# A stick-breaking row's survival product in one scan against a floor tile, and the residual gate's sum moved behind the last such row

## The chip, the cores and the metric

The kernel runs on one core of a Trainium2 chip. The metric is the device time of one execution in microseconds (us): a median of three executions. Engines are named as the profile names them: PE (TensorE, matrix multiplication), DVE (VectorE), ACT (ScalarE), POOL (GpSimd) and SP (SyncE, which here issues DMAs).

## The reference

One layer with two groups of eight heads of 64 columns, over 1024 positions of width 1024. What matters here is the stick-breaking group and the residual's gate:

```python
def _stick_breaking_block(q, k, v, q_pos, k_pos):
    z = einsum('bhqd,bhkd->bhqk', q, k) * scale
    strict = k_pos[None, :] < q_pos[:, None]
    log_beta = log_sigmoid(z)
    log_keep = where(strict, log_sigmoid(-z), 0.0)
    later = cumsum(log_keep, axis=3, reverse=True) - log_keep
    w = where(strict, exp(log_beta + later), 0.0)
    return einsum('bhqk,bhkd->bhqd', w, v)
...
mod = silu(c) @ w_ada + b_ada          # shift, scale, gate: 1024 columns each
u = layer_norm(x) * (1 + scale) + shift
h = u @ w_in                           # q, k, v, g and forget columns of both groups
y = concat([y_fox, y_sb]) @ w_out      # heads' outputs times silu of their g columns
x = layer_norm(2 ** 0.25 * x + gate * y, ln_g, ln_b)
```

The other group, forgetting attention, is an ordinary causal softmax with a bias of cumulated forget gates.

## The kernel before

All matrix products are made of float32 split into a high and a low part (`whi`/`wlo`, `uh`/`ul`, `pt` in two halves), three matmuls for one.

*Start.* The sequence is normalised, and the projection of the first two pairs of heads is made while the modulation is worked out. In this stage, w_gate comes in as eight tiles of 128 x 1024 (`wg`, in the `att` ring of six buffers), and DVE adds them up, each times its element of silu(c), into the tile `gate` (`gate_term`, 16 halves). Two matmuls with a constant 0.5 sum that tile over its partitions, and b_gate is added (`gen_gate`).

*Attention.* Eight pairs of heads follow one another. Pairs 0 to 3 are stick-breaking, pairs 4 to 7 forgetting. A unit is one pair, one head and one block `i` of 128 queries, against (i+1) x 128 keys. For a stick-breaking unit: PE makes the scores S, ACT makes `kp` = sigmoid(-S) and `be` = sigmoid(S), DVE turns `kp` from right to left into the product of all later keeps with two scans, first on the 128 diagonal columns (against `ident`, whose one restarts the product at each row's own position), then on the columns left of them, starting from the first scan's last value. POOL multiplies `be` by the shifted `kp`. Two units later PE transposes the result, ACT and DVE split it (`pt`), and PE multiplies it by v (`pv`). The score tile has one buffer, so the next unit's scores wait for ACT's two sigmoids. For a forgetting unit DVE adds the bias row `fb` and reduces, ACT takes the exponential, DVE inverts the sum and POOL scales the row (`a`).

*Fillers.* Between the units' matmuls PE works through `fillers`, a chain of generators that make the projections of later pairs in small steps (`gen_m`: `m` tiles for q, k or g of a pair, `gen_v`: v of two pairs). `FILL` tells how many steps each pair's units take with them. `beside(main, side)` advances `side` by one step for each step of `main`. `gen_split_out` runs beside pairs 4 to 6: it loads half a block of w_out, multiplies it by `gate` (`raw_o`, L123), splits it (`whi_o` L125, `wlo_o` L126) and stores both parts in DRAM (`wo_dr`), from where `gen_last_g` loads them for the output projection. `SPACE` is the number of steps between two of the 16 halves. All weights pass through two `raw` buffers (`raw_tile`) and a ring of five pairs of `whi`/`wlo` buffers (`RING`).

*Order.* PE's order is that of the code, and SP's is in the start stage; the other queues, and SP later, are ordered by a scheduler. Each engine works through its own queue in order.

Of the kernel before, what the change touches and what calls it, by code (L numbers as in the profile page):

```python
# [13 lines left out]
P = 128  # L14
# [13 lines left out]
def tile_hybrid_layer(  # L28
# [27 lines left out]
    def att_tile(name, dt=F32):  # L56
        return big("att", 6, name, dt)
# [18 lines left out]
    GEARLY = 8  # L76
    NORM_ON = {6: nc.vector, 7: nc.vector}
    FROW = 12
    SPACE = 5
    GATE = 6  # L80
# [23 lines left out]
    gate = cp.tile([P, D], F32, tag="gate", name="gate")  # L104
# [292 lines left out]
    def att_scores(u, following):  # L397
# [28 lines left out]
        else:  # L426
# [6 lines left out]
            rv = kp[:, dg][:, ::-1]  # L433
            nc.vector.tensor_tensor_scan(rv, rv, ident[:, ::-1], initial=0.0, op0=ALU.mult, op1=ALU.max)  # L434
            if i:
                rv = kp[:, :ke - P][:, ::-1]
                nc.vector.tensor_tensor_scan(rv, rv, rv, initial=kp[:, ke - P:ke - P + 1],  # L437
                                             op0=ALU.mult, op1=ALU.min)
# [51 lines left out]
    def chain(gens):  # L490
        for g in gens:
            yield from g
# [179 lines left out]
    wg = {}  # L672

    def load_gate(kt):
        wg[kt] = att_tile(f"wg_{kt}")
        nc.sync.dma_start(wg[kt], w_gate[kt])

    def gate_term(kt, h):
        s = slice(h * 512, h * 512 + 512)
        if kt == 0:  # L680
            nc.vector.tensor_scalar(gate[:, s], wg[kt][:, s], sc[:, 0:1], None, op0=ALU.mult)
        else:
            nc.vector.scalar_tensor_tensor(gate[:, s], wg[kt][:, s], sc[:, kt:kt + 1], gate[:, s],
                                           op0=ALU.mult, op1=ALU.add)

    def gen_gate():
        b = att_tile("bg")
        nc.sync.dma_start(b, b_gate.to_broadcast([P, D]))
        for _ in range(GATE):
            yield  # L690
        for h in range(2):
            s = slice(h * 512, h * 512 + 512)
            gp = t_tile(f"gate_{h}")

            nc.tensor.matmul(gp, half.to_broadcast([P, P]), gate[:, s], start=True, stop=True)
            nc.vector.scalar_tensor_tensor(gate[:, s], b[:, s], 0.5, gp, op0=ALU.mult, op1=ALU.add)
            yield
# [21 lines left out]
    for kb in range(NB):  # L719
        if kb + 2 < NB:  # L720
            rounded = late_round(kb + 2)
        start_steps(range(2), acc1, kb, 512, 1024)
        if kb < 4:
            load_gate(kb)
        if kb < len(evacs):
            n, h = evacs[kb]
            with after(*rounded):
                evac_m(*START[n], 0, acc0[n], (h,))
    acc1 += [pv_tile("st_g0b"), pv_tile("st_q1b"), acc_tile("st_k1b")]
    v0_w.update((n, fetch_w(f"v0_{n}b", w_v[0, n], 512)) for n in (2, 3))  # L730
    for n in range(5):
        if n >= 2:
            for kb in range(NB):
                start_steps((n,), acc1, kb, 512, 1024)
                step = (n - 2) * NB + kb
                if step % 3 == 1 and step // 3 < GEARLY:
                    with after(rounded[1]):
                        gate_term(step // 3, 0)
                        gate_term(step // 3, 1)
                    if step // 3 < 4:  # L740
                        load_gate(step // 3 + 4)
        last_evac = evac_m(*START[n], 1, acc1[n])
# [22 lines left out]
    def gen_split_out():  # L765
        for pr in range(NPAIR):
            for h in range(2):
                s = slice(h * 512, h * 512 + 512)
                hi, lo = fetch_w(f"o{pr}_{h}", w_out[pr * P:(pr + 1) * P, s], 512, gate[:, s])
# [97 lines left out]
    def gen_last_g(p):  # L867
# [14 lines left out]
        beside(chain([gen_v(0, v0_w, range(4, NB)), gen_m(1, 2)]), gen_gate()),  # L882
# [142 lines left out]
```

## Time and profile before

| | |
|---|---|
| executions | 709.02, 707.76, 707.51 us; median 707.76 |
| span of the profiled execution | 705.8 us, clock 0.998 |
| time of the profiled execution itself | not recorded apart from its span; the median lies 1.96 us above it |
| PE / DVE / ACT / POOL busy | 680.8 / 509.6 / 378.8 / 422.4 us |
| first score of attention | 92.6 us |
| first scores of pairs 1, 2, 3, 4 | 148.1, 222.8, 292.1, 361.7 us |
| first scores of pairs 5, 6, 7 | 435.5, 508.1, 571.3 us |

The span runs from the first to the last instruction of one profiled execution. PE is busy for 96% of it, so the interest lies in the few microseconds in which it is not, and in what it waits for then. In the views a group of instructions is named by its line, its engine and operation and the tiles it writes and reads (out<-in), then its count, its busy time, the mean of one in ns, and the engine's idle time just before it with what ended that.

### The profile page before, as it was taken

To read this page: it belongs to the slowest core of one execution; us is meant where nothing else is said; L and a number is where in the kernel's file an instruction comes from. 1 tells how busy PE (TensorE), PEld (TensorE's weight loads), DVE (VectorE), ACT (ScalarE), POOL (GpSimd) and SP (SyncE) were. 2 spreads that over 40 slices of the span, in tenths; PEclk is the share of its full clock that TensorE was granted. 3 is DMA by queue.
4 is the path that set the end of the run, shared out by engine and by line. 5 is a ranking of instruction groups with operands and counts; after the bars stand their busy time and mean duration, and the time that the engine had idled before them with its cause. 6 is when DMAs were issued, how large, how long until landed. Compare 5 with 4: busy or idle time off the path is not lost. (4 is left out here: it accounts for less than half of the span.)

```text
span 705.8 us, 11791 instructions
## 1 busy us (share of the span) xinstructions
PE 680.8 (96%) x4033; PEld 593.0 (84%) x4033; DVE 509.6 (72%) x963; ACT 378.8 (54%) x856; POOL 422.4 (60%) x523
## 2 busy tenths in 40 slices
PE   7999998989999999999999999999999999999995
PEld 4789887878998888889998887889988889888884
DVE  5985689897858697788686685757676767774644
ACT  4667346756658566666665563646564666621000
POOL 4560258665629675857388897868583455665412
PEclk9999999999999999999999999999999999999999
DMA  8953451101101212112034554435241189143301
GB/s 306 415 212 126 132 167 35 28 26 53 53 7 37 70 37 67 43 38 68 9 124 155 176 170 137 134 105 165 92 148 53 56 271 371 48 162 113 121 32 59
DMA packets 44027, 81.59 MB, mean 116 GB/s; under 512 B 5120, under 2 KB 18880, under 8 KB 43072
## 3 DMA queue, kind: packets, MB, share of 16 engines
q1 hardware_dynamic: 42816, 76.65, 32.4%
q10 hardware_dynamic: 1152, 4.19, 2.1%
q8 instruction: 32, 0.52, 0.3%
q14 instruction: 27, 0.22, 0.1%
HBM read 60.34 MB, written 16.29 MB: 109 GB/s over the span
## 5 line engine op out<-in xcount | busy, mean ns | idle before, releaser
L256 PE MATMUL m<-uh,whi 128*128 128x512 f32 x304 | 126.4, 416 | 0.0
L257 PE MATMUL m<-ul,whi 128*128 128x512 f32 x304 | 119.9, 394 | 0.0
L258 PE MATMUL m<-uh,wlo 128*128 128x512 f32 x304 | 119.7, 394 | 0.0
L459 DVE TENSOR_TENSOR pt<-T,pt 128x512 fp32r<-128x512 f32 (+2 forms) x192 | 100.5, 549 | 14.6 <-ACT pt L458 13.3
L439 POOL TENSOR_TENSOR be<-be,kp 128x127 f32<-128x127 f32 (+3 forms) x64 | 79.0, 1235 | 47.0 <-DVE kp L437 44.3
L458 ACT CAST pt<-T 128x512 fp32r<-128x512 f32 (+2 forms) x192 | 85.8, 480 | 18.6 <-PE T L456 14.8
L471 PEld LDWEIGHTS pv<-pt,v 128*128 128x128 f32 x640 | 83.9, 188 | 10.4 <-DVE pt L459 5.2
L471 PE MATMUL pv<-pt,v 128*128 128x256 f32 (+1 forms) x640 | 85.1, 277 | 4.5 <-DVE pt L459 3.6
L437 DVE TENSOR_TENSOR_SCAN kp<-kp 128x128 f32<-128x128 f32 (+6 forms) x56 | 82.6, 1476 | 1.9
L424 POOL TENSOR_SCALAR a<-a,l 128x1024 f32<-128x1024 f32 (+3 forms) x64 | 48.3, 755 | 41.7 <-DVE l L423 28.1
L422 ACT ACTIVATE a<-a,nm 128x1024 f32<-128x1024 f32 (+3 forms) x64 | 49.8, 779 | 40.8 <-DVE nm L417 38.9
L410 PE MATMUL S<-k,q 128*128 128x512 f32 (+5 forms) x192 | 66.8, 349 | 2.3 <-ACT be L430 1.7
L258 PEld LDWEIGHTS m<-uh,wlo 128*128 128x128 f32 x304 | 57.1, 188 | 13.6
L411 PE MATMUL S<-kl,qz 128*128 128x512 f32 (+5 forms) x192 | 65.5, 342 | 0.0
L256 PEld LDWEIGHTS m<-uh,whi 128*128 128x128 f32 x304 | 57.3, 189 | 8.8 <-DVE kl L244 0.4
L257 PEld LDWEIGHTS m<-ul,whi 128*128 128x128 f32 x304 | 57.4, 189 | 8.0
L480 POOL TENSOR_TENSOR ty<-ty,sg 64x256 f32<-64x256 f32 x64 | 48.8, 762 | 19.7 <-DVE ty L479 9.8
L434 DVE TENSOR_TENSOR_SCAN kp<-kp,ident 128x128 f32<-128x128 f32 x64 | 42.0, 656 | 24.4 <-ACT kp L429 21.1
L417 DVE CUSTOM_DVE_ANT_0 a<-S,fb 128x1024 f32<-128x1024 f32 (+3 forms) x64 | 48.2, 754 | 15.7 <-issue 6.5
L429 ACT ACTIVATE kp<-S 128x128 f32<-128x128 f32 (+3 forms) x64 | 41.7, 652 | 32.9 <-PE S L411 31.4
L126 POOL TENSOR_TENSOR wlo<-raw,whi 128x512 fp32r<-128x512 f32 x38 | 56.8, 1496 | 3.4 <-DMA wo_dr<-wlo_o 1.8
L311 PE MATMUL v<-whi_v,uh 128*128 128x256 f32 (+1 forms) x192 | 56.0, 292 | 1.1 <-DVE kl L244 1.1
(280 smaller groups left out, 1633.2 us busy)
## 6 DMA issues: line engine op xcount, KB each, us to landing
raw<-in_w_qkg_dram SPq DMA_DIRECT2D x38, 256.0 KB, 2.7
wss<-in_w_ss_dram SPq DMA_DIRECT2D x7, 1024.0 KB, 8.5
x<-in_x_dram SPq DMA_DIRECT2D x8, 512.0 KB, 7.6
k<-k SPq DMA_DIRECT2D x32, 128.0 KB, 2.2
wg<-in_w_gate_dram SPq DMA_DIRECT2D x8, 512.0 KB, 5.2
raw_o<-in_w_out_dram SPq DMA_DIRECT2D x16, 256.0 KB, 2.6
fb<-f_dr ACTq DMA_DIRECT2D x8, 512.0 KB, 4.2
wo_dr<-whi_o SPq DMA_DIRECT2D x16, 256.0 KB, 2.5
```

Of the source, the lines that this page charges most:

```text
L126: nc.gpsimd.tensor_tensor(lo[:, :n], raw, hi.bitcast(F32)[:, :n], op=ALU.subtract)
L256: nc.tensor.matmul(acc, hi[:, c], u_hi[kt][:, s], start=(kt == 0), stop=False)
L257: nc.tensor.matmul(acc, hi[:, c], u_lo[kt][:, s], start=False, stop=False)
L258: nc.tensor.matmul(acc, lo[:, c], u_hi[kt][:, s], start=False, stop=(kt == NB - 1))
L311: nc.tensor.matmul(acc[:, :n], u_hi[kt][:, ts_], hi[:, s], start=(kt == 0), stop=False)
L410: nc.tensor.matmul(S[:, s, :w], qst[p][h][:, qs], kst[p][h][:, ks], start=True, stop=False)
L411: nc.tensor.matmul(S[:, s, :w], z, klo[p][:, ks], start=False, stop=True)
L437: nc.vector.tensor_tensor_scan(rv, rv, rv, initial=kp[:, ke - P:ke - P + 1], op0=ALU.mult, op1=ALU.min)
L439: nc.gpsimd.tensor_tensor(be[:, :ke - 1], be[:, :ke - 1], kp[:, 1:ke], op=ALU.mult)
L458: nc.scalar.copy(hi[:, :n, qo:qo + P], t3)
L459: nc.vector.tensor_tensor(lo[:, :n, qo:qo + P], t3, hi.bitcast(F32)[:, :n, qo:qo + P], op=ALU.subtract)
L471: nc.tensor.matmul(acc[:, q0:256], vt[p][:, kb, h * P:(h + 1) * P], pt[:, kb % 4, q0:], start=(part == 0 and kb == 0), stop=(part == 1 and ...
```

## The change

The two scans of a stick-breaking row become one over the whole row. Its second operand is a new tile `floor`, 1024 columns wide: zeros, and `ident` in the last 128. The state is multiplied by `kp` and then held at no less than the floor. POOL writes `floor` at the start.

`floor` lies in the buffer of `gate` (both have the tag `gate` in a pool with one buffer). The gate can therefore only be begun when the last stick-breaking scan has read `floor`. The sum moves from the start stage into `gen_gate`, which now runs beside the fillers of pairs 4 and 5: 16 halves of 128 x 512, loaded through the two `raw` buffers, one every `GATE` = 2 steps after `GATE0` = 6 steps, then the two matmuls. `gen_split_out` follows behind it, beside the fillers from pair 6's k on, with `SPACE` 3 instead of 5.

```diff
-    GEARLY = 8
...
-    SPACE = 5
-    GATE = 6
+    SPACE = 3
+    GATE0 = 6
+    GATE = 2
...
-    gate = cp.tile([P, D], F32, tag="gate", name="gate")
+    floor = cp.tile([P, D], F32, tag="gate", name="floor")
+    nc.gpsimd.memset(floor[:, :D - P], 0.0)
+    nc.gpsimd.tensor_copy(floor[:, D - P:], ident)
...
-            rv = kp[:, dg][:, ::-1]
-            nc.vector.tensor_tensor_scan(rv, rv, ident[:, ::-1], initial=0.0, op0=ALU.mult, op1=ALU.max)
-            if i:
-                rv = kp[:, :ke - P][:, ::-1]
-                nc.vector.tensor_tensor_scan(rv, rv, rv, initial=kp[:, ke - P:ke - P + 1],
-                                             op0=ALU.mult, op1=ALU.min)
+            rv = kp[:, :ke][:, ::-1]
+            nc.vector.tensor_tensor_scan(rv, rv, floor[:, D - ke:][:, ::-1], initial=0.0,
+                                         op0=ALU.mult, op1=ALU.max)
...
-    def load_gate(kt):
-        wg[kt] = att_tile(f"wg_{kt}")
-        nc.sync.dma_start(wg[kt], w_gate[kt])
...
     def gen_gate():
-        b = att_tile("bg")
-        nc.sync.dma_start(b, b_gate.to_broadcast([P, D]))
-        for _ in range(GATE):
+        for _ in range(GATE0):
             yield
+        gate = cp.tile([P, D], F32, tag="gate", name="gate")
+        gates.append(gate)
+        for kt in range(NB):
+            for h in range(2):
+                s = slice(h * 512, h * 512 + 512)
+                raw = raw_tile(f"wg_{kt}_{h}")[:, :512]
+                nc.sync.dma_start(raw, w_gate[kt][:, s])
+                if kt == 0:
+                    nc.vector.tensor_scalar(gate[:, s], raw, sc[:, 0:1], None, op0=ALU.mult)
+                else:
+                    nc.vector.scalar_tensor_tensor(gate[:, s], raw, sc[:, kt:kt + 1], gate[:, s],
+                                                   op0=ALU.mult, op1=ALU.add)
+                for _ in range(GATE):
+                    yield
         for h in range(2):
             s = slice(h * 512, h * 512 + 512)
+            b = raw_tile(f"bg_{h}")[:, :512]
+            nc.sync.dma_start(b, b_gate[:, s].to_broadcast([P, 512]))
             gp = t_tile(f"gate_{h}")
             nc.tensor.matmul(gp, half.to_broadcast([P, P]), gate[:, s], start=True, stop=True)
-            nc.vector.scalar_tensor_tensor(gate[:, s], b[:, s], 0.5, gp, op0=ALU.mult, op1=ALU.add)
+            nc.vector.scalar_tensor_tensor(gate[:, s], b, 0.5, gp, op0=ALU.mult, op1=ALU.add)
             yield
...
-        beside(chain([gen_v(0, v0_w, range(4, NB)), gen_m(1, 2)]), gen_gate()),
+        gen_v(0, v0_w, range(4, NB)), gen_m(1, 2),
...
-        beside(chain([gen_m(4, 2), gen_m(5, 0), gen_m(5, 1), gen_m(5, 2),
-                      gen_m(6, 0), gen_m(6, 1), gen_v(3), gen_m(6, 2),
-                      gen_m(7, 0), gen_m(7, 1)]), gen_split_out()),
+        beside(chain([gen_m(4, 2), gen_m(5, 0), gen_m(5, 1), gen_m(5, 2), gen_m(6, 0)]), gen_gate()),
+        beside(chain([gen_m(6, 1), gen_v(3), gen_m(6, 2), gen_m(7, 0), gen_m(7, 1)]), gen_split_out()),
```

DVE's queue at the end of the start stage and through the first three units of pair 0, before (`kl` and `q` are the low part of k and the shared half of q for pair 1; `kp` with `ident` is the diagonal scan):

```order
L683 SCALAR_TENSOR_TENSOR gate<-wg_844,sc,gate 128x512
L683 SCALAR_TENSOR_TENSOR gate<-wg_857,sc,gate 128x512
L233 SCALAR_TENSOR_TENSOR q_1_252<-st_q1b,q_1_252 64x512
L683 SCALAR_TENSOR_TENSOR gate<-wg_857,sc,gate 128x512
L683 SCALAR_TENSOR_TENSOR gate<-wg_872,sc,gate 128x512 x2
L244 TENSOR_TENSOR kl_255<-st_k1b,k_0_253 64x512
L244 TENSOR_TENSOR kl_255<-st_k1b,k_1_254 64x512
L434 SCALAR_TENSOR_TENSOR kp_0_0_940<-kp_0_0_940,ident 128x128
L320 TENSOR_TENSOR v_523<-v_4_950,v_523 128x128
L434 SCALAR_TENSOR_TENSOR kp_0_1_982<-kp_0_1_982,ident 128x128
L437 SCALAR_TENSOR_TENSOR kp_0_1_982<-kp_0_1_982 128x128
```

The same place in the changed kernel:

```order
L235 SCALAR_TENSOR_TENSOR q_0_253<-st_q1b,q_0_253 64x512
L235 SCALAR_TENSOR_TENSOR q_1_254<-st_q1b,q_1_254 64x512
L246 TENSOR_TENSOR kl_257<-st_k1b,k_0_255 64x512
L246 TENSOR_TENSOR kl_257<-st_k1b,k_1_256 64x512
L436 SCALAR_TENSOR_TENSOR kp_0_0_910<-kp_0_0_910,floor 128x128
L322 TENSOR_TENSOR v_525<-v_4_918,v_525 128x128
L436 SCALAR_TENSOR_TENSOR kp_0_1_950<-kp_0_1_950,floor 128x256
```

The gate terms are gone from between `q` and `kl`, and one scan over all columns stands where two stood.

DVE's queue at pair 4's third and fourth units, before (L417 is the score reduction, `sg` the gate projection's evacuation):

```order
L417 ISA a_0_5_4324,nm_0_5_4325<-S_0_5_4319,fb_4133 128x768
L417 ISA nm_0_5_4325 128x1
L250 SCALAR_TENSOR_TENSOR sg_4228<-sg_4228,m_2_1_4229 128x512
L395 TENSOR_TENSOR fb_4133<-fb_4133,causal 128x128
L423 RECIPROCAL l_0_5_4326<-l_0_5_4326 128x1
L479 TENSOR_TENSOR ty_1_3_4372<-pv_1_3_4355,ty_1_3_4372 64x256
L459 TENSOR_TENSOR pt_4_0_3_0_4378<-T_0_7_0_4379,pt_4_0_3_0_4377 128x4x128
```

In the changed kernel:

```order
L419 ISA a_0_5_4221,nm_0_5_4222<-S_0_5_4216,fb_4040 128x768
L419 ISA nm_0_5_4222 128x1
L252 SCALAR_TENSOR_TENSOR sg_4125<-sg_4125,m_2_1_4126 128x512
L688 SCALAR_TENSOR_TENSOR gate<-wg_1_4528,sc,gate 128x512
L397 TENSOR_TENSOR fb_4040<-fb_4040,causal 128x128
L425 RECIPROCAL l_0_5_4223<-l_0_5_4223 128x1
L478 TENSOR_TENSOR ty_1_3_4264<-pv_1_3_4247,ty_1_3_4264 64x256
L458 TENSOR_TENSOR pt_4_0_3_0_4270<-T_0_7_0_4271,pt_4_0_3_0_4269 128x4x128
L458 TENSOR_TENSOR pt_4_0_3_1_4279<-T_0_7_1_4280,pt_4_0_3_1_4278 128x4x128
L688 SCALAR_TENSOR_TENSOR gate<-wg_0_4559,sc,gate 128x512
```

Gate terms, each of which waits for its load, now stand about twice in each unit between the reductions and the `pt` operations; the last of the 16 stands at the reduction of the second head's second row.

POOL's queue behind the last v weights of pairs 6 and 7 (`whi_v`/`wlo_v` 3), before (`a` with L424 is a row's scaling, `ty` the attention output times its g part, `whi`/`wlo` 2_0 weights of pair 6's g):

```order
L126 TENSOR_TENSOR wlo_v_3_5543<-raw_v_3_5540,whi_v_3_5542 128x512
L424 TENSOR_SCALAR a_0_0_5487<-a_0_0_5487,l_0_0_5489 128x128
L125 TENSOR_SCALAR whi_o_1_5578<-raw_o_1_5575 128x512
L126 TENSOR_TENSOR wlo_o_1_5579<-raw_o_1_5575,whi_o_1_5578 128x512
L123 TENSOR_TENSOR raw_o_0_5711<-raw_o_0_5711,gate 128x512
L125 TENSOR_SCALAR whi_o_0_5714<-raw_o_0_5711 128x512
L126 TENSOR_TENSOR wlo_o_0_5715<-raw_o_0_5711,whi_o_0_5714 128x512
L424 TENSOR_SCALAR a_1_7_5551<-a_1_7_5551,l_1_7_5553 128x1024
```

In the changed kernel, further on among the rows of pair 5's second head:

```order
L426 TENSOR_SCALAR a_1_5_5575<-a_1_5_5575,l_1_5_5577 128x768
L127 TENSOR_SCALAR whi_o_1_5616<-raw_o_1_5613 128x512
L479 TENSOR_TENSOR ty_0_0_5627<-ty_0_0_5627,sg_4785 64x256
L125 TENSOR_TENSOR raw_o_0_5719<-raw_o_0_5719,gate 128x512
L128 TENSOR_TENSOR wlo_o_1_5617<-raw_o_1_5613,whi_o_1_5616 128x512
L426 TENSOR_SCALAR a_1_4_5668<-a_1_4_5668,l_1_4_5670 128x640
L127 TENSOR_SCALAR whi_o_0_5722<-raw_o_0_5719 128x512
L128 TENSOR_TENSOR wlo_o_0_5723<-raw_o_0_5719,whi_o_0_5722 128x512
L125 TENSOR_TENSOR raw_o_1_5835<-raw_o_1_5835,gate 128x512
L426 TENSOR_SCALAR a_1_3_5731<-a_1_3_5731,l_1_3_5733 128x512
L127 TENSOR_SCALAR whi_o_1_5838<-raw_o_1_5835 128x512
```

There is now nearly one split for every row `a` here; the first of the 16 stands behind the row of pair 5's third unit, and the last of the 16 stands behind the weights of pair 7's k, among the rows of pair 6's second head.

More of the change, by code (lines that the diff above doesn't have):

```diff
@@ L670, in tile_hybrid_layer @@
             make_v(0)
[L672 to L684 removed]
+    gates = []
     def gen_gate():
[L687 to L689 removed]
+        for _ in range(GATE0):
             yield
+        gate = cp.tile([P, D], F32, tag="gate", name="gate")
[12 more added lines that the diff above has]
+                    yield
         for h in range(2):
             s = slice(h * 512, h * 512 + 512)
+            b = raw_tile(f"bg_{h}")[:, :512]
+            nc.sync.dma_start(b, b_gate[:, s].to_broadcast([P, 512]))
             gp = t_tile(f"gate_{h}")
             nc.tensor.matmul(gp, half.to_broadcast([P, P]), gate[:, s], start=True, stop=True)
[L696 removed]
+            nc.vector.scalar_tensor_tensor(gate[:, s], b, 0.5, gp, op0=ALU.mult, op1=ALU.add)
             yield
@@ L734, in tile_hybrid_layer @@
                 start_steps((n,), acc1, kb, 512, 1024)
[L735 to L741, printed above, removed]
         last_evac = evac_m(*START[n], 1, acc1[n])
@@ L768, in gen_split_out @@
                 s = slice(h * 512, h * 512 + 512)
-                hi, lo = fetch_w(f"o{pr}_{h}", w_out[pr * P:(pr + 1) * P, s], 512, gate[:, s])
+                hi, lo = fetch_w(f"o{pr}_{h}", w_out[pr * P:(pr + 1) * P, s], 512, gates[0][:, s])
                 nc.sync.dma_start(wo_dr[0, pr, :, s], hi.bitcast(F32)[:, :512])
```

2 lines of the change are left out of this document (removed).

## The prediction

> **What bounds the kernel now.** First the page's busy times.
>
> ```profile
> PE 680.8 (96%) x4033; PEld 593.0 (84%) x4033; DVE 509.6 (72%) x963; ACT 378.8 (54%) x856; POOL 422.4 (60%) x523
> ```
>
> PE (TensorE) does the work of nearly the whole span: a change on DVE (VectorE) or POOL (GpSimd) can win only what PE stands idle, and can lose whatever it makes PE wait. So the second view is the busy time by stage. Attention runs from 92.5 to 571 us, in eight pairs of heads; the first four rows are the stick-breaking pairs 0 to 3, the other four the forgetting pairs 4 to 6.
>
> ```profile
> core 0: us, PE busy (x) PEld busy (x) DVE busy (x) ACT busy (x) POOL busy (x), PEclk, DMA share, GB/s
> 92.50:148.00 55.50, 49.32 (x319) 43.31 (x318) 48.96 (x70) 37.10 (x86) 42.97 (x50) 1.00 0.19 55
> 148.00:222.50 74.50, 72.94 (x495) 67.33 (x494) 57.31 (x96) 44.77 (x103) 41.38 (x53) 1.00 0.14 37
> 222.50:292.00 69.50, 68.73 (x387) 59.04 (x387) 55.04 (x76) 46.95 (x100) 49.49 (x62) 1.00 0.18 50
> 292.00:361.50 69.50, 69.28 (x482) 64.23 (x480) 54.01 (x88) 43.67 (x102) 42.18 (x54) 1.00 0.18 52
> 361.50:449.00 87.50, 85.97 (x483) 74.31 (x482) 60.05 (x131) 47.91 (x114) 76.99 (x83) 1.00 0.49 157
> 449.00:473.00 24.00, 24.00 (x143) 20.90 (x142) 14.21 (x37) 13.47 (x34) 14.80 (x19) 1.00 0.28 82
> 473.00:509.00 36.00, 35.95 (x295) 35.43 (x294) 25.13 (x66) 20.21 (x58) 25.02 (x28) 1.00 0.39 123
> 509.00:546.50 37.50, 37.44 (x214) 32.20 (x212) 25.30 (x61) 20.20 (x49) 22.57 (x27) 1.00 0.37 117
> ```
>
> PE's idle time is the stretch less the second number: 6.2 us in pair 0, then 1.6, 0.8, 0.2; and 1.5 in pair 4. In pair 0 DVE is busy 48.96 of 55.5 us (88%), in pair 1 57.31 of 74.5 (77%). The clock is 1.00 throughout and is no part of this. Third, PE's waits from 92 to 362 us: line, whom it waited for, total, times, longest.
>
> ```profile
> PE pv L471 <- DVE pt L459: 2.1, 4, 1.3
> PE S L410 <- ACT be L430: 1.7, 1, 1.7
> PE T L456 <- POOL wlo_v L126: 1.6, 1, 1.6
> PE T L456 <- DVE pt L459: 1.2, 1, 1.2
> PE v L311 <- DVE kl L244: 1.1, 1, 1.1
> PE pv L471 <- ACT pt L458: 0.7, 1, 0.7
> PE T L456 <- POOL be L440: 0.2, 1, 0.2
> ```
>
> These are 8.6 us, and most end on DVE. That is the most that relief in the stick-breaking pairs can win.
>
> **Gate terms taken out of the start.** DVE just before attention (start, us, what):
>
> ```profile
> 91.46 0.69 DVE L233 SCALAR_TENSOR_TENSOR q<-st_q1b,q 64x512 fp32r<-64x512 f32 x1
> 92.19 3.46 DVE L683 SCALAR_TENSOR_TENSOR gate<-wg,sc,gate 128x512 f32<-128x512 f32 x3
> 95.68 0.68 DVE L244 TENSOR_TENSOR kl<-st_k1b,k 64x512 fp32r<-64x512 f32 x1
> 97.01 0.69 DVE L244 TENSOR_TENSOR kl<-st_k1b,k 64x512 fp32r<-64x512 f32 x1 [0.65 <-ACT k L241]
> ```
>
> Three gate terms hold up kl, kl holds up ACT's copy of k, and behind that in ACT's queue stand the sigmoids of the first unit, for which PE's second score (L410) waits 1.7 us. Without the 3.46 us the wait is covered twice over: I count all 1.7. What is late next is PE itself, which then has its queue to work through.
>
> **One scan for two.**
>
> ```profile
> L437 DVE TENSOR_TENSOR_SCAN kp<-kp x56: 482/1284/2984, 99.0 to 360.9; 128x128 f32<-128x128 f32 x8, 128x256 f32<-128x256 f32 x8, 128x384 f32<-128x384 f32 x8, 128x512 f32<-128x512 f32 x8
> L437 DVE TENSOR_TENSOR_SCAN kp<-kp 128x384 f32<-128x384 f32 x8 | 8.1, 1018 | 0.3
> L434 DVE TENSOR_TENSOR_SCAN kp<-kp,ident x64: 405/426/1949, 97.7 to 360.2; 128x128 f32<-128x128 f32 x64
> L434 DVE TENSOR_TENSOR_SCAN kp<-kp,ident 128x128 f32<-128x128 f32 x64 | 42.0, 656 | 24.4 <-ACT kp L429 21.1 <-POOL be L439 1.5 <-ACT qz L388 1.0
> ```
>
> The shortest second scan, 128 columns, takes 482 ns and 384 columns 1018: 268 ns for each 128. The diagonal scan has the form of the new one (two different tiles), with a median of 426. So a row of i+1 blocks goes from 426 + 482 + 268(i-1) to 426 + 268i: 214 ns less for each of the 56 rows with i>0, 12.0 us in all. Nothing says that two tiles are slower than one, so it doesn't go below that. Above: the mean of L434 lies 230 ns over its median, a wait at the start. [...] By the rows, L437 would give up at most its whole excess, 82.6 us (page) less 56 unhindered scans (8 x 9.0 us), 10.6 us.
>
> ```profile
> L437 DVE TENSOR_TENSOR_SCAN kp<-kp 128x128 f32<-128x128 f32 (+6 forms) x56 | 82.6, 1476 | 1.9
> ```
>
> So DVE is relieved by 12.0 to 22.6 us over four pairs; I take the low end, since a POOL operation already running costs the same wait whichever scan meets it. Pair 0 loses 14 x 0.21 = 3.0, the three gate terms 3.5 and two closing gate operations 1.3 us: 41.2 us in some 50 of pair 0, 82% at most, near pair 1's 77%, where PE idles 2%. At that 2% pair 0 keeps 1.1 of its 6.2 idle us: 5.1 gained, the 1.7 above among them. Of the 2.6 us in pairs 1 to 3 I take half, 1.4 (one of them, 0.7, waits for ACT alone). **Gain 6.5**, between 1.7 and 8.6.
>
> The floor costs two POOL operations at the start. The nearest row, a memset of 128 columns, takes 0.2 us, so 896 columns at most 7 x 0.2 = 1.4; POOL stands idle there for longer, until the first statistics come:
>
> ```profile
> L172 POOL TENSOR_SCALAR rs_a<-mv_a 128x1 f32<-128x1 f32 x8 | 2.2, 270 | 7.8 <-DVE mv_a L170 7.5
> L92 POOL MEMSET causal<- 128x128 f32 x1 | 0.2, 204 | 0.0
> ```
>
> Counted at nothing. PE's two gate matmuls move, and cost the same.
>
> **The gate sum in pair 4.**
>
> ```profile
> 361.50:408.00 46.50, 46.50 (x269) 40.57 (x268) 32.45 (x70) 26.11 (x61) 41.64 (x44) 1.00 0.47 153
> L683 DVE SCALAR_TENSOR_TENSOR gate<-wg,sc,gate x14: 743/750/1770, 75.2 to 93.9; 128x512 f32<-128x512 f32 x14
> L681 DVE TENSOR_SCALAR gate<-wg,sc x2: 479/480/481, 74.4 to 74.8; 128x512 f32<-128x512 f32 x2
> PE pv L471 <- DVE pt L459: 1.5, 1, 1.5
> DVE fb L395 <- DMA fb<-f_dr: 3.6, 1, 3.6
> ```
>
> 14 x 0.75 + 2 x 0.48 = 11.5 us go into about these 46.5, where DVE was busy 32.45: 44 of 46.5, 95%. Each of the 16 loads now waits on SP (the DMA queue) for one of two raw buffers, which it shares with the weight halves; DVE waits for the load, and behind it in DVE's queue stand pt and the score reductions, for which PE waits. What a DMA wait of DVE costs here is shown: 3.6 us on fb (last two rows, 362 to 571 us) became 1.5 us on PE, so the slack is about 2 us. [...] Bounds: 0, if each load comes within that slack, and 4, if two or three overrun like fb. I take **1.2**.
>
> **The output weights' splits in pairs 5 and 6.**
>
> ```profile
> L123 POOL TENSOR_TENSOR raw_o<-raw_o,gate 128x512 f32<-128x512 f32 x5 | 6.5, 1298 | 3.6 <-DMA raw_o<-in_w_out_dram 3.6
> L125 POOL TENSOR_SCALAR whi_o<-raw_o 128x512 fp32r<-128x512 f32 x5 | 3.1, 619 | 0.8 <-PE m L257 0.7
> L126 POOL TENSOR_TENSOR wlo_o<-raw_o,whi_o 128x512 fp32r<-128x512 f32 x5 | 6.5, 1304 | 2.3 <-DMA wo_dr<-wlo_o 2.2
> L126 POOL TENSOR_TENSOR wlo<-raw,whi 128x512 fp32r<-128x512 f32 x8 | 10.4, 1300 | 1.1 <-DMA wo_dr<-wlo_o 0.7
> L123 POOL TENSOR_TENSOR raw_o<-raw_o,gate x16: 1282/1294/1354, 333.7 to 497.2; 128x512 f32<-128x512 f32 x16
> ```
>
> The first four rows are of 449 to 546.5 us. A split costs POOL 1.30 + 0.62 + 1.30 = 3.22 us. Before, the 16 ran from 334 to 497 us (last row). Now the first follows the gate, whose closing operations stand in DVE's new order beside pair 5's second and third rows, which I put at about 447 us; the last stands, in POOL's order, by the weights that PE wants at 546.5 (pair 7's k). In the three rows from 449 to 546.5 POOL was busy 62.4 us, 5 splits (16.1) among them; with 16 it is 62.4 + 11 x 3.22 = 97.8 of 97.5 us. Behind the half that PE wants first stand three weight halves and the last split, 3 x 1.92 + 3.22 = 9.0, so 88.8 us must fit: 91%. The fullest long stretch before, 361.5 to 449, had 88% and no PE wait on POOL. At 88% it would take 100.9, 3.4 us late; at 91% nothing. I take **2.0**. What may hide it is that PE transposes a normalised row two units after its scores; if POOL runs later than that, PE waits for the row as well as for the weights.
>
> **Sum.** Against the profiled execution: 705.8 - 6.5 + 1.2 + 2.0 = 702.5 us of span. The median shown is 707.76, 1.96 above the span (what lies around it, and one execution against another), so **704.4 us**; with 0.2% (1.4 us) as what a measurement of this kernel can tell from no change, that is faster.
>
> **Rivals.** *POOL becomes the bound between 449 and 546.5 us* (slower). For it: splits share the ring of five weight buffers with the v weights of pairs 6 and 7, which hold four of them from 473 to 509 us, so each waits for the store of the one before; in the rows above five splits bring 3.6 + 2.2 us of DMA waits, 1.2 each. If 15 splits carry that unhidden, POOL takes 88.8 + 17.4 = 106.2 us, 8.7 late. Against it: in 361.5 to 449 ten splits ran beside everything else and PE did not wait. Price: 705.8 - 6.5 + 1.2 + 8.7 = 709.2, 711.2 as a median. It decides above 0.9 us of wait for each split, where the lateness passes the gain left.
> *The waits of pair 0 are not DVE's alone*: POOL's product be is next in the chain and POOL is busy 42.97 of 55.5 us there. Then only the 1.7 goes, and pairs 4 to 6 pay between 0 and 3.2; at the middle, 1.6, the time is 707.7, no change.
> *Everything stays covered*: 8.6 less the ACT wait of 0.7 is won and nothing paid: 705.8 - 7.9 + 1.96 = 699.9.
>
> **Chances.** Forecast 0.55, POOL bound 0.22, no relief 0.12, all covered 0.11. Faster: 0.52 of the first and 0.11, 0.63. Same: 0.03 and 0.10, 0.13. Slower: 0.22 and 0.02, 0.24. The range goes from the covered case, 699, to just past the POOL case, 712; the forecast's own range, with the bounds of pairs 4 to 6, is 701 to 707.
>
> **What would show it.** Right: no L410 wait at 97 us; pair 0 some 5 us shorter; scans at 426 + 268i ns; PE waits in pair 4 under 2 us and from 449 to 546.5 on POOL's weights or rows under 4. Wrong: DVE waiting for wg again and again and PE behind it; POOL above 95% busy with PE waiting on wlo; or pair 0 as long as before with PE waiting on be.

## The result, and the profile after

The changed kernel takes 714.21 us (median of 4 executions), the kernel before 707.88 on the same chip: a ratio of 1.0084, 95% interval 1.0060 to 1.0109. It is slower; the prediction said 704.4 and faster. The profiled span grew from 705.8 to 712.0 us.

The quickest way to see where is to follow one mark through both programs: the first score matmul of each pair. From the timelines, before (L410) and after (L412), the first scores of pairs 4 and 5 (start, us, what):

```profile
361.75 0.48 PE L410 MATMUL S<-k,q 128*128 128x512 f32 x1
435.54 0.47 PE L410 MATMUL S<-k,q 128*128 128x512 f32 x1
```
```profile
355.12 0.48 PE L412 MATMUL S<-k,q 128*128 128x512 f32 x1
437.62 0.48 PE L412 MATMUL S<-k,q 128*128 128x512 f32 x1
```

At pair 4 the changed kernel is 6.6 us ahead. Pair 4 then takes 82.5 us instead of 73.8, and the whole lead is lost in it and 2.1 us more. The same marks for every run of this study, us against the kernel before (negative is earlier), with the measured times. The marks come from one profiled execution of each kernel, the medians from 4 to 12. The profiled one lay within 1.7 us of the median, but for x1 (718.43, the fastest of six), x2 (709.07, the slowest of twelve) and x5 (718.93, the slowest of six). The ratio is to the kernel before in the same series of runs, where its median was 707.58 to 708.77:

| kernel | at pair 4 | at pair 5 | at pair 7 | median, us | ratio, interval |
|---|---|---|---|---|---|
| changed | -6.6 | +2.1 | +6.9 | 714.21 | 1.0084, 1.0060 to 1.0109 |
| g1, move alone | +0.5 | +7.8 | +12.5 | 719.67 | 1.0175, 1.0154 to 1.0196 |
| g2, terms without loads | -6.4 | +0.5 | +7.0 | 712.04 | 1.0056, 1.0037 to 1.0075 |
| g3, one term | -7.2 | -7.6 | -3.4 | 705.34 | 0.9965, 0.9950 to 0.9979 |
| g4, splits without product | -7.0 | +1.6 | +3.2 | 711.01 | 1.0045, 1.0030 to 1.0060 |
| g5, terms spread, no loads | -6.9 | -6.3 | -0.8 | 705.99 | 0.9967, 0.9954 to 0.9981 |
| g6, terms spread, loads ahead | -6.7 | +5.5 | +14.1 | 720.11 | 1.0168, 1.0145 to 1.0192 |
| x1, gate at the end | -7.3 | -7.1 | +10.1 | 721.90 | 1.0195, 1.0163 to 1.0227 |
| x2, loads in the ring | -7.0 | -6.1 | +2.1 | 706.88 | 0.9981, 0.9969 to 0.9992 |
| x3, gate at the end, ring | -6.6 | -7.0 | +6.0 | 715.14 | 1.0103, 1.0086 to 1.0120 |
| x4, x2 with the gate at the end | -6.7 | -5.8 | -4.1 | 704.42 | 0.9940, 0.9925 to 0.9955 |
| x5, x2 with splits earlier | -7.2 | -6.2 | +11.9 | 714.66 | 1.0098, 1.0072 to 1.0124 |
| x7, ring, terms not held | -6.8 | -2.7 | +2.5 | 709.29 | 1.0014, 0.9998 to 1.0030 |

What pair 4 waits for, in the views of waits of the changed kernel from 355 to 450 us (engine, line, whom it waited for: total us, times, longest):

```profile
PE S L412 <- DVE nm L419: 4.5, 2, 3.3
PE pv L470 <- DVE pt L458: 2.1, 2, 1.2
```
```profile
DVE gate L688 <- DMA wg<-in_w_gate_dram: 13.0, 10, 3.2
```
```profile
SPq L684 <- DMA wg<-in_w_gate_dram: 8.8, 6, 2.6
SPq L684 <- POOL wlo L128: 7.5, 5, 1.9
SPq L684 <- DVE gate L688: 5.6, 6, 1.5
```

Read from the bottom: SP cannot issue a gate load (L684) until one of the two raw buffers is free, so it waits for POOL's weight splits, for DVE's last term and for earlier gate loads to land; DVE waits 13.0 us for the loads; PE waits 6.6 us for DVE. The worst place in the timeline, DVE first, then PE:

```profile
374.59 1.29 DVE L458 TENSOR_TENSOR pt<-T,pt 128x512 fp32r<-128x512 f32 x2
379.11 0.94 DVE L688 SCALAR_TENSOR_TENSOR gate<-wg,sc,gate 128x512 f32<-128x512 f32 x1 [3.23 <-DMA wg<-in_w_gate_dram]
379.97 0.81 DVE L419 CUSTOM_DVE_ANT_0 a<-S,fb 128x640 f32<-128x640 f32 x1
```
```profile
376.63 0.93 PE L455 MATMUL T<-ident,a 128*128 128x128 f32 x7
380.84 0.79 PE L412 MATMUL S<-k,q 128*128 128x512 f32 x1 [3.28 <-DVE nm L419]
```

The row reduction (L419) needs nothing from the gate, but stands behind a gate term in DVE's queue, and the score tile that it would free has one buffer. The stretches of 3.41 us around that wait show a second loss (the PEclk column, behind POOL's):

```profile
core 0: us, PE busy (x) PEld busy (x) DVE busy (x) ACT busy (x) POOL busy (x), PEclk, DMA share, GB/s
377.28:380.69 3.41, 0.28 (x3) 0.04 (x1) 1.58 (x2) 0.00 (x0) 2.06 (x3) 1.00 0.25 77
380.69:384.10 3.41, 3.26 (x8) 2.58 (x9) 1.69 (x6) 2.44 (x6) 0.80 (x1) 0.50 0.42 154
384.10:387.51 3.41, 2.51 (x21) 2.32 (x20) 3.41 (x9) 0.84 (x3) 0.42 (x1) 1.00 0.46 149
```

After a stretch in which PE did almost nothing, its granted clock was 0.50 for 3.41 us, which is 1.7 us of work lost. Pair 4's 8.7 us are thus 6.6 us more idle time of PE between the two marks (6.7 against 0.1, the gaps of the timeline added up), 1.7 us of half clock and 0.4 of other things.

In the first four pairs the first-unit wait at 97 us is gone; the scans and the floor (duration ns min/median/max; first and last start):

```profile
L436 DVE TENSOR_TENSOR_SCAN kp<-kp,floor x64: 412/1568/3704, 95.3 to 353.0; 128x128 f32<-128x128 f32 x8, 128x256 f32<-128x256 f32 x8, 128x384 f32<-128x384 f32 x8, 128x512 f32<-128x512 f32 x8
L105 POOL MEMSET floor<- x1: 844/844/844, 2.3 to 2.3; 128x896 f32 x1
```
```profile
L436 DVE TENSOR_TENSOR_SCAN kp<-kp,floor 128x128 f32<-128x128 f32 (+3 forms) x64 | 105.1, 1643 | 32.0 <-ACT kp L431 31.5
```

In pair 6 the waits for weight halves appear that the prediction had weighed (511 to 579 us), with POOL busy 86.8 of 97.5 us from 449 to 546.5:

```profile
PE m L258 <- POOL whi L127: 1.5, 1, 1.5
PE m L260 <- POOL wlo L128: 1.3, 3, 0.6
PE T L455 <- POOL a L426: 0.4, 1, 0.4
```
```profile
449.00:546.50 97.50, 95.96 (x633) 86.83 (x632) 66.69 (x162) 52.97 (x137) 86.80 (x94) 1.00 0.53 174
```

### The profile page after: what moved, and what is told of

Read it like the earlier page. It is cut to its first block, busy times and chain, and to the rows that moved or that the text cites. A ratio compares the mean times of both kernels' runs of the same rounds, so it can differ in the third digit from the quotient of the medians.

```text
span 712.0 us, 11737 instructions
## 1 busy us (share of the span) xinstructions
PE 684.0 (96%) x4033; PEld 595.3 (84%) x4033; DVE 490.2 (69%) x907; ACT 379.3 (53%) x856; POOL 431.6 (61%) x525
## 4 chain that ended last, share of the span: by engine, by line
PE 74%; DMA 9%; DVE 6%; POOL 5%; issue 3%; ACT 2%; SPq 0%; POOLq 0%; DVEq 0%; ACTq 0%
PE pv L470 8%; PE m L260 7%; PE m L258 7%; PE m L259 7%; PE T L455 7%; PE o L806 4%; PE o L804 4%; PE o L805 4%; PE v L313 3%; PE v L315 3%; PE v L314 3%; PE S L413 3%; PE S L412 3%; DMA wg<-in_w_gate_dram 2%; DMA raw<-in_w_qkg_dram 2%
## 5 line engine op out<-in xcount | busy, mean ns | idle before, releaser
L258 PE MATMUL m<-uh,whi 128*128 128x512 f32 x304 | 127.1, 418 | 1.5 <-POOL whi L127 1.5
L436 DVE TENSOR_TENSOR_SCAN kp<-kp,floor 128x128 f32<-128x128 f32 (+3 forms) x64 | 105.1, 1643 | 32.0 <-ACT kp L431 31.5
L424 ACT ACTIVATE a<-a,nm 128x1024 f32<-128x1024 f32 (+3 forms) x64 | 49.8, 778 | 48.9 <-DVE nm L419 48.3
L412 PE MATMUL S<-k,q 128*128 128x512 f32 (+5 forms) x192 | 67.3, 352 | 4.5 <-DVE nm L419 4.5
L258 PEld LDWEIGHTS m<-uh,whi 128*128 128x128 f32 x304 | 57.7, 190 | 10.6 <-POOL whi L127 1.8
L479 POOL TENSOR_TENSOR ty<-ty,sg 64x256 f32<-64x256 f32 x64 | 53.9, 841 | 14.0 <-DVE ty L478 9.0
L419 DVE CUSTOM_DVE_ANT_0 a<-S,fb 128x1024 f32<-128x1024 f32 (+3 forms) x64 | 48.2, 753 | 17.6 <-PE S L413 6.0
L128 POOL TENSOR_TENSOR wlo<-raw,whi 128x512 fp32r<-128x512 f32 x38 | 55.2, 1454 | 2.6 <-DVE l L425 0.7
L390 ACT CAST qz<-q 64x128 fp32r<-64x128 f32 x128 | 37.4, 295 | 33.4 <-PE S L413 32.1
```

Of the source, the lines that this page charges most:

```text
L128: nc.gpsimd.tensor_tensor(lo[:, :n], raw, hi.bitcast(F32)[:, :n], op=ALU.subtract)
L258: nc.tensor.matmul(acc, hi[:, c], u_hi[kt][:, s], start=(kt == 0), stop=False)
L412: nc.tensor.matmul(S[:, s, :w], qst[p][h][:, qs], kst[p][h][:, ks], start=True, stop=False)
L436: nc.vector.tensor_tensor_scan(rv, rv, floor[:, D - ke:][:, ::-1], initial=0.0, op0=ALU.mult, op1=ALU.max)
```

## The experiments: where the loss is

**Theory A**: DVE waits for gate loads, PE behind it, then the half clock. **Theory B**: DVE has no room for 11.5 us of terms in pair 4. **Theory C**: the loss is the splits' on POOL. The first four kernels take one thing each from the changed kernel.

**g1, the move without the scan.** The old two scans, no floor; the rest as changed.

```diff
-    floor = cp.tile([P, D], F32, tag="gate", name="floor")
...
-            nc.vector.tensor_tensor_scan(rv, rv, floor[:, D - ke:][:, ::-1], initial=0.0,
-                                         op0=ALU.mult, op1=ALU.max)
+            nc.vector.tensor_tensor_scan(rv, rv, ident[:, ::-1], initial=0.0, op0=ALU.mult, op1=ALU.max)
...
+                nc.vector.tensor_tensor_scan(rv, rv, rv, initial=kp[:, ke - P:ke - P + 1],
+                                             op0=ALU.mult, op1=ALU.min)
```

> The gate's sum stands where the changed kernel has it (pair 4, 16 loads through the two raw buffers; output-weight splits denser behind it), but each stick-breaking row keeps its two scans and there is no floor. This parts the two halves of the change. In the changed kernel the units run 2.4 us earlier than before at the first unit, and 6.6 to 7.0 earlier at pair 4; the start's part (2.4) stays here, the scan's part (4.2 to 4.6) should go. All theories put the loss in pairs 4 to 6, so all expect 714.2 + 4.4 = 718.6 us (716.5 to 720.5). If it comes out at 714 or below, the scan won nothing, and the loss is smaller than the traces say.

Measured 719.67. The scan is worth 5.5 us of the time, 7.1 us at pair 4 (+0.5 against -6.6). What was not expected: without it the move wins nothing in the first four pairs. The fifth and the ninth unit start 2.4 and 3.2 us earlier there too, but then PE waits 2.9 us for pt until 119.2 us, and the mean granted clock of the profiled execution is 0.989 (changed kernel 0.993). In DVE's queue the two scans of one row, 4.9 us together, stand ahead of that pt. From 92 to 150 us:

```profile
PE pv L470 <- DVE pt L458: 3.1, 2, 2.9
```

**g2, the terms without their loads.**

```diff
-                raw = raw_tile(f"wg_{kt}_{h}")[:, :512]
-                nc.sync.dma_start(raw, w_gate[kt][:, s])
+                raw = u_hi[kt].bitcast(F32)[:, s]
```

> The changed kernel, with the 16 gate terms still on DVE in pair 4, of the same form and size, but each reading a 512-column half of the activations' tile, which has been in SBUF since the start, and not a loaded piece of the gate's weights: the 16 loads are left out, so the gate is another. Theory A (DVE waits for the loads: 13.0 us of waits in the trace, PE behind it, and then the half clock) expects the loss of pair 4 to go, some 9 to 10 us: 704 to 706 us, DVE with no wait for a gate load, PE with no wait over 2 us in pair 4 and the clock at 1.00 there. Theory B (DVE is simply full: 11.5 us of terms put into a stage where it had little room) expects at most 2 us of it back: 712 to 714. Theory C (the loss is the output-weight splits' on POOL) expects 711 to 714 too.

Measured 712.04, which is what theory B expected. But the trace shows another kernel than was meant. Without loads to wait for, the scheduler put the first four terms together in DVE's queue, ahead of the split of pair 3's last transposes (DVE, then what PE made of it):

```profile
355.72 2.02 DVE L685 TENSOR_SCALAR gate<-uh,sc 128x512 f32<-128x512 f32 x2
357.66 0.28 DVE L322 TENSOR_TENSOR v<-v,v 128x128 fp32r<-128x128 f32 x1
357.87 3.99 DVE L687 SCALAR_TENSOR_TENSOR gate<-uh,sc,gate 128x512 f32<-128x512 f32 x2
361.78 1.01 DVE L458 TENSOR_TENSOR pt<-T,pt 128x512 fp32r<-128x512 f32 x2
```
```profile
PE pv L470 <- DVE pt L458: 3.9, 1, 3.9
```

The granted clock was at half for 6.8 us after it (its mean over the execution is 0.989). The four terms took 6.0 us here, where the unhindered ones of the kernel before make 2 x 0.48 + 2 x 0.75 = 2.5. So this run doesn't decide between A and B; it shows that the place of the terms in DVE's queue can cost nearly as much as late loads do (pair 4 is 6.9 us longer than before, with the loads 8.7).

**g3, one term of eight.**

```diff
+                if kt:
+                    for _ in range(GATE):
+                        yield
+                    continue
```

> The changed kernel with the gate's sum cut to its first of eight pieces (2 loads and 2 terms in the place of 16 and 16; the bias, the two matmuls and the splits behind them stay), so the gate is another. This takes away both the waits and DVE's work in pair 4. Theory A expects the same as without the loads, within 1 us: 703.5 to 705.5. Theory B expects the loss of pair 4 to go only here: 703.5 to 705.5, against 712 to 714 for the kernel that keeps the terms and drops the loads. Theory C expects 711 to 714, since the splits stay as dense.

Measured 705.34. Waits and work of the gate sum together cost 8.9 us; theory C is out as the main cause, since the splits are as dense here.

**g4, splits without the product by the gate.**

```diff
-                hi, lo = fetch_w(f"o{pr}_{h}", w_out[pr * P:(pr + 1) * P, s], 512, gates[0][:, s])
+                hi, lo = fetch_w(f"o{pr}_{h}", w_out[pr * P:(pr + 1) * P, s], 512)
```

> The changed kernel, with the 16 output-weight splits left without their product by the gate (16 POOL operations of 1.3 us gone, 20.8 us of POOL between 449 and 565 us; the output is not gated then). The gate's sum in pair 4 stays. Theories A and B, which put 7 to 10 us of the loss into pair 4, expect only what the trace shows from 480 to 565 us back, PE's waits of some 2.9 us for weight halves and up to 1 us of rows: 710.5 to 712. Theory C (POOL's splits are the loss) expects 704 to 707.

Measured 711.01, 3.2 us back: the weight-half waits are gone, those for nm stay.

**g5, g2 with the terms spread.** Each term is held in DVE's queue behind the newest row's reduction:

```diff
-            nc.vector.tensor_tensor_reduce(out=v3(a), in0=S[:, :ns, :w], in1=v3(f),
+            row_dve[0] = nc.vector.tensor_tensor_reduce(out=v3(a), in0=S[:, :ns, :w], in1=v3(f),
...
+                with after(row_dve[0]):
+                    nc.vector.scalar_tensor_tensor(gate[:, s], raw, sc[:, kt:kt + 1], gate[:, s],
+                                                   op0=ALU.mult, op1=ALU.add)
```

> As the kernel with terms and no loads (712.0 us), but each gate term is held in DVE's queue behind the newest row's reduction at its place, so that the 16 terms stand one behind each row of pair 4 and no longer bunch: there, five stood ahead of the last row's pt from 355.7 to 361.8 us, PE waited 3.9 us and the clock halved for 6.8. The loads are left out, so the gate is another. Theory A (the waits for the loads are the loss) expects what one term alone gave, 705.3 us, within 1.5: 704 to 706.8. Theory B (DVE has no room for 11.5 us of terms in pair 4) expects the loss to stay wherever the terms stand: 709 to 712.

Measured 705.99. (Of the terms that bunched in g2, the trace has four ahead of that pt, not five.) All 16 terms are there (12.8 us of DVE, from 367.6 us on), and from 355 to 450 us PE waits once:

```profile
PE pv L471 <- DVE pt L459: 0.4, 1, 0.4
```

So theory B is wrong: DVE had the room. The loss in pair 4 needs the waits for the loads, or terms placed ahead of what PE waits for. This run takes both away; x2 and x7 below part them as far as they can be parted.

## The experiments: can the loads be had for less?

**g6, the whole gate again: terms held as in g5, each two steps behind its load.**

```diff
                 nc.sync.dma_start(raw, w_gate[kt][:, s])
+                yield
+                yield
+                with after(row_dve[0]):
```

> The whole computation: the changed kernel, with each gate term held behind a row's reduction as in the kernel beside this one, and two steps of PE's order behind its own load instead of directly behind it. If the loads' lateness is the loss (theory A), the 13.0 us of DVE waits fall to under 4, PE's waits in pair 4 to under 2, and the time is 705 to 708. If the two raw buffers are the limit (a load held longer keeps a weight half out), PE waits for weight halves in pair 4 instead: 709 to 713. Theory B expects 710 to 714.

Measured 720.11, worse than the changed kernel. DVE's waits for loads fell from 13.0 to 3.9 us, and PE waits for DVE no more; it waits for weights (355 to 450 us):

```profile
PE m L258 <- POOL whi L127: 7.3, 4, 2.6
PE m L260 <- POOL wlo L128: 1.6, 3, 0.6
```

A gate piece that comes in earlier holds one of the two raw buffers longer, and the weight halves pass through the same two; with other buffers (x2) these waits in pair 4 are gone. The mean granted clock was 0.987 (changed kernel 0.993).

**x1, the gate multiplied in at the end.** Splits without the gate from the kernel before's place on (the first stands at 353 us), gate terms through pairs 4 to 6, still through the raw buffers.

```diff
+        nc.vector.tensor_tensor(r[:, s], o_acc[t, h][:, :s.stop - s.start], gates[0][:, s], op=ALU.mult)
+        nc.vector.scalar_tensor_tensor(r[:, s], xr[:, s], ALPHA, r[:, s], op0=ALU.mult, op1=ALU.add)
```

> The whole computation in another place: the one scan and its floor stay; the output weights are split without the gate, from the place where the kernel before began them (334 us) and five steps apart; the gate terms go one by one through pairs 4 to 6, five steps apart, each two steps behind its load and behind a row's reduction; the gate multiplies the finished accumulators at the end (one more DVE operation for each of the 17 halves, where DVE is busy 15 to 19 of 30 us). If DVE's queue in pair 4 and POOL's between 449 and 565 us are where the changed kernel loses, both losses go: 707.9 - 7 (gain up to pair 4) + 0.6 (one more operation behind the last matmul) = 701.5 us (700 to 704.5). If the last stage has less room than that, or the gate's loads hinder the weights' through the two raw buffers, 705 to 709.

Measured 721.90, a miss: splits, weights and gate pieces share the two buffers, and PE waits for weight halves from 355 to 510 us (then 17 us at half clock; its mean over the execution is 0.985):

```profile
PE v L315 <- POOL wlo_v L128: 3.9, 3, 2.2
PE v L313 <- POOL whi_v L127: 3.0, 1, 3.0
PE m L258 <- POOL whi L127: 2.7, 1, 2.7
```

**x2, the gate's loads in the ring.** One pair of the ring's five takes both halves of a piece, loaded two steps ahead of its first term; terms held as in g5.

```diff
+            pair = [t.bitcast(F32)[:, :512] for t in ring_w(f"wg_{kt}")]
+            for h in range(2):
+                nc.sync.dma_start(pair[h], w_gate[kt][:, h * 512:h * 512 + 512])
```

> The whole computation, the changed kernel's order, with one thing altered: the gate's weights no longer pass through the two raw buffers, but are loaded into a pair of the ring of weight buffers (8 pairs, both 512-column halves of one piece in a pair), three to four steps of PE's order ahead of their two terms, which are held behind a row's reduction in DVE's queue. If what the held-back loads cost was the two raw buffers (the kernel with terms spread and loads ahead gave 720.1, PE waiting for weight halves 2.0 + 0.9 + 2.6 + 1.8 us; without loads the same order gave 706.0), this gives 706 to 708, with no PE wait over 1 us on a weight half or on nm between 361 and 450 us. If the ring (five pairs) is as short as the raw buffers, the weights' splits come late in the same way: 710 to 720.

Measured 706.88. From 355 to 450 us DVE waits for no gate load and PE only 1.1 us; the waits for weight halves in pair 6 stay (505 to 575 us):

```profile
PE m L258 <- POOL whi L127: 3.0, 2, 1.7
PE m L260 <- POOL wlo L128: 1.3, 2, 0.6
```

**x7, the ring without holding the terms.** Against x2:

```diff
-                with after(row_dve[0]):
```

> The whole computation: the gate's loads in the ring, as in the kernel that gave 706.9, but the terms not held behind the rows' reductions: they stand in DVE's queue where the changed kernel has them. This parts the two edits. If the loads alone were the trouble: 706 to 708. If the terms' place in DVE's queue (ahead of the rows' pt and nm, as where five of them bunched) costs as well: 709 to 713.

Measured 709.29: of the 7.3 us between the changed kernel and x2, the other buffers with the earlier loads give 4.9, and holding the terms 2.4. The second number isn't the place in the queue alone, since DVE still waits 4.3 us for gate loads here, and not at all in x2. The first two terms stand ahead of pt's two halves from 357 to 361 us, which costs PE 2.1 us.

**x3, x1 with the gate's loads in the ring.** x2's lines in x1, each piece three steps ahead of its first term, with four steps behind each term (`GATE = 4`).

> The whole computation: the gate multiplied into the finished accumulators at the end, splits without it from 334 us on and five steps apart, as in the kernel that gave 721.9, but the gate's weights loaded into pairs of the ring, eight steps apart, and not through the raw buffers. In that kernel PE waited for weight halves 2.7 us in pair 4 and 0.8 + 3.0 + 0.9 + 2.2 us at 472 to 483 us and the clock halved for 17 us behind them. If that was the raw buffers' doing, these go and the time is 701 to 704.5. If the ring of five, which splits, weights and gate pieces now share, is the limit, PE's waits for weight halves stay: 709 to 722.

Measured 715.14. With the ring 6.8 us of x1's time are gone, not all of its loss. One long wait remains, at 508 us: in SP's queue the loads of two weight halves stand behind stores of y and of split weights and go out at 502.1 and 503.3 us, POOL waits 3.9 us for the first of them to be split, and PE for POOL. No run tried why they go out so late.

```profile
PE m L258 <- POOL whi L127: 5.7, 1, 5.7
```

**x5, x2 with the splits right behind the gate.**

```diff
-        beside(chain([gen_m(4, 2), gen_m(5, 0), gen_m(5, 1), gen_m(5, 2), gen_m(6, 0)]), gen_gate()),
-        beside(chain([gen_m(6, 1), gen_v(3), gen_m(6, 2), gen_m(7, 0), gen_m(7, 1)]), gen_split_out()),
+        beside(chain([gen_m(4, 2), gen_m(5, 0), gen_m(5, 1), gen_m(5, 2),
+                      gen_m(6, 0), gen_m(6, 1), gen_v(3), gen_m(6, 2),
+                      gen_m(7, 0), gen_m(7, 1)]), chain([gen_gate(), gen_split_out()])),
```

> The whole computation: the kernel with the gate's loads in the ring, its splits beginning right behind the gate's last operation (some 5 of PE's 98 steps earlier) and not with the weights of pair 6's k; same spacing of three, same product. If POOL's late weight halves at 529 to 548 us come from the splits' being pressed against the end, an earlier start takes away some 5 of 53 steps of pressing, two to three us of POOL's lateness and with them one of the two half-clock stretches: 703 to 706. If it is POOL's load and not the place, no change: 706 to 708.

Measured 714.66, a miss: the waits did not shrink, they moved (the profile is of the slowest execution). The earlier splits meet the v weights of pairs 6 and 7 at 471 us, and another weight half comes late at 537 (440 to 575 us):

```profile
PE v L313 <- POOL whi_v L127: 3.2, 2, 2.9
PE m L258 <- POOL whi L127: 3.2, 1, 3.2
```

**x4, x2 with the gate at the end.** The splits stay in the changed kernel's place, without the product (g4's edit); x1's two operations close each half.

> The whole computation: the kernel with the gate's loads in the ring (706.9), with the splits where they are, but without their product by the gate (20.8 us of POOL gone), and the gate multiplied into the finished accumulators by one more DVE operation for each of 17 halves. In the kernel with loads in the ring PE still waits 1.3 + 0.6 + 1.7 + 0.6 us for weight halves at 529 to 548 us, with the clock at half for 6.8 us (3.4 lost): 7.6 at most to be had. Where the changed kernel lost its split's product alone, 3.2 us came back. If POOL is what is late there: 706.9 - 3.2 to 6 + 0.6 for the operation at the end = 701.5 to 704.5. If the end pays more than 0.6 (DVE between 640 and 700 us), 704.5 to 707.

Measured 704.42, ratio 0.9940 (0.9925 to 0.9955): it beats both kernels, the one before by 0.6%. No wait for a weight half is left from 505 to 575 us:

```profile
PE S L413 <- DVE nm L420: 0.9, 1, 0.9
PE T L456 <- POOL a L427: 0.3, 1, 0.3
```

The operation at the end costs more than the 0.6 put down for it: between pair 7's first score and the end of the span this kernel loses 0.9 us (from -4.1 to -3.2), where x2 wins 0.6 (from +2.1 to +1.5).

## Why the prediction was wrong

**The gain of 6.5: right in size, half luck in kind.** The first scores of pair 4 come 6.6 us earlier. Pair 0 got 4.5 us shorter (5.1 predicted), pairs 1 to 3 2.0 (1.4). But the term stood for PE's idle time, and that fell less. From pair 0's first score to pair 4's, before and after (columns as above; PE's busy time is the second number, what is left of the first is idle):

```profile
92.58:361.75 269.17, 260.44 (x1680) 234.13 (x1678) 215.50 (x328) 172.74 (x389) 176.26 (x216) 1.00 0.17 48
92.45:355.12 262.67, 258.88 (x1675) 234.39 (x1674) 194.10 (x266) 173.27 (x390) 177.21 (x210) 0.99 0.17 46
```

The idle time fell by 4.9 us, from 8.7 to 3.8, and a half clock in pair 0 took 1.7 of that back: PE still waits 1.9 us for pt until 113.3 us, and from 114.5 us the clock is 0.50 for 3.41 us. The other 3.3 us are work that PE no longer has in this stretch. The gate's two matmuls (two records each) have moved from pair 0 to pair 5:

```profile
L695 PE MATMUL gate<-gate,half x4: 590/592/592, 105.3 to 109.5; 128*128 128x512 f32 x4
L697 PE MATMUL gate<-gate,half x4: 590/591/592, 442.5 to 446.0; 128*128 128x512 f32 x4
```

The prediction said rightly that they cost the same there. So a part of the lead at pair 4 is only work put off; how much of the 3.3 us is theirs was not measured alone.

The L410 wait is gone, as predicted. The shortest scans of each width take 412 ns for 128 columns to 2292 for 1024, 426 + 268i within 4%. DVE's scans fell from 124.6 to 105.1 us, by 19.5, nearer the upper end of 12.0 to 22.6: besides the 12.0 of the arithmetic, the time above the unhindered scans fell by 7.5. In the two timelines of DVE and POOL all but 0.6 us of such time lies in scans that began while a POOL operation was running: before, 67 of the 120 scans began so and took 25.1 us more in all than the shortest of their line and width, after, 40 of the 64 and 18.5 us; each of the others was within 21 ns of the shortest. The longest diagonal scan, 1.95 us, began at 146.03 us, and the POOL operation that ran then (L439, 1.78 us from 145.92) had 1.67 us left. So fewer starts met such an operation, which the low end left out; no run separates this from the rest of the change.

**The gate sum in pair 4: the step that failed.** It was put at 1.2 us, between 0 and 4; it cost 8.7. Its DVE work was judged rightly: 95% busy was taken as bearable, and g5, with the same terms, is only 0.6 us slower than g3 with two of them. The loads were not.

```profile
wg<-in_w_gate_dram SPq DMA_DIRECT2D x15, 256.0 KB, 2.9
```

The step took the slack of 2 us from one wait on fb (3.6 us on DVE, 1.5 on PE) as something that each of the 16 loads would find anew. That wait and its 1.5 us lie at 434 to 440 us, where pair 5 begins; in pair 4 itself PE idled only 0.1 us before. In the changed kernel the loads take 2.9 us in the median from issue to landing (the view of DMA issues, 355 to 450 us; count, KB each, median us). They stand directly ahead of their terms, and ten of the waits on them, 13.0 us together, came one behind the other in a queue that was to be 95% full. With these waits the prediction's own sum gives the size: 32.45 us of DVE work, 11.5 of terms and 13.0 of waits make 57 us in a stretch of 46.5, 10.5 too many, where pair 4 lost 8.7. The 13.0 stands in the changed kernel's trace alone. The prediction named the sign ("DVE waiting for wg again and again and PE behind it") and priced it at a seventh.

**The half clock was not in the sum at all.** "The clock is 1.00 throughout and is no part of this" was true of the kernel before alone, up to its last 3 us. Pair 4's waits cost 1.7 us more than their length, pair 0's wait 1.7 of the gain: together 3.4 of the 6.1 us by which the span grew.

**The splits: right.** Put at 2.0 (0 to 3.4). By the marks the changed kernel loses 4.0 us from pair 5's first score to the end: 1.2 in pair 5, 3.7 in pair 6, and 0.8 won behind that. The 1.2 are not the splits': in pair 5, where the gate's matmuls came in, PE's idle time fell from 1.5 to 1.1 us and its busy time rose by 1.6. In pair 6 the idle time rose by 2.7 us (0.5 to 3.2), and taking the product away gave 3.2 back. POOL was busy 86.8 us where 88.8 had to fit.

**The sum by the marks**: 705.8 - 6.6 + 8.7 + 4.0 = 711.9 us, against a span of 712.0. These are differences of two profiles, so they must add up; what they show is where the time went.

**The rivals.** *POOL as the bound* was priced at 711.2, not far from the result, but for a loss of 8.7 in pairs 5 and 6, which was some 3; the time came from elsewhere. *Pair 0's waits not DVE's alone* allowed 1.7 us; PE's idle time in pair 0 fell by 3.5 (6.2 to 2.7), so it is wrong. *Everything covered* failed with the loads. No rival had the gate's loads as its mechanism, although the text held all its parts; that is why the range ended 2 us below the result.

## What to carry to other kernels

A load that stands directly ahead of its use in an in-order queue can stop that queue until it lands, each time anew: here 16 loads of 2.9 us gave ten waits and 13.0 us. The landing times, less the work that stands between, are the bound to price it by, not the slack that a single wait had found. Before more loads go through a shared buffer, ask what else passes through it: fetching ahead helped only once the gate had other buffers (720.1 against 706.9). A side sum is cheap when its terms stand behind the operation for which the critical engine waits, and dear ahead of it (2.4 us here, late loads included), and a factor on an output can wait until an engine has room (x4, 2.5 us below x2). And a mark that comes earlier isn't yet a gain: look whether the critical engine idles less, or whether work has moved behind the mark.

## What the hardware showed that was not expected

PE's granted clock fell to half after short waits. In the changed kernel's trace it was 0.50 for 3.41 us twice ahead of the last matmul, from 114.45 and from 380.69 us. In the 3.41 us just before, PE was busy 1.54 us (111.04 to 114.45, with a single wait of 1.9 us) and 0.28 us (377.28 to 380.69). These two starts and that of the half clock at the end, 708.37 us, lie 78 and 96 times 3.413 us apart. In the kernel before, with stretches of 3.413 us counted back from its one change of the clock, at 702.61 us, PE was busy only 1.73 us in the one from 95.04 and 1.77 in the one from 142.83, and the clock was 1.00 in both and in the next. Between 1.54 and 1.73 us the two traces have no such stretch. The half clock did not always last 3.41 us: in g2 it lasted 6.8, and in g4, around 382 us, some 6.8 too. While it lasted in the changed kernel, a 512-column matmul took 628 ns instead of 414 (L258, 381 to 384 us and 390 to 400 us):

```profile
L258 PE MATMUL m<-uh,whi 128*128 128x512 f32 x2 | 1.3, 628 | 0.0
L258 PE MATMUL m<-uh,whi 128*128 128x512 f32 x11 | 4.6, 414 | 0.0
```

The trace before had no such stretch until its last 3 us, and the prediction left the clock out. A wait that is new should be priced with it: here each of the two stretches cost 1.7 us on top.
